# An encoder layer in split fp32 on one core: first loads of the down stages in another order, low parts of the weights on another engine

## The chip, the cores and the metric

The kernel runs on one core of a Trainium2 chip. The metric is the time of one execution on the device in microseconds (us), lower is better. A time of the kernel is the median of three runs. Beside the runs there is one profiled execution, with a trace of every instruction; its times are told from the start of its span.

The engines of the core have these names in the profile: PE is TensorE (PEld its loading of the stationary operand), DVE is VectorE, ACT is ScalarE, POOL is GpSimd, SP is SyncE, which here only issues DMAs. A name with a q behind it (SPq, ACTq) is the DMA queue of that engine.

## The reference

One layer of an encoder is applied to two groups of rows, 256 and 512 tokens (768 rows together), with the same weights. D is 1024, D_FF 2816.

```python
def swiglu(x, w_gu, w_down):
    gate, up = jnp.split(x @ w_gu, 2, axis=-1)
    return (jax.nn.silu(gate) * up) @ w_down
...
x = layer_norm(DN_ALPHA * x + 0.5 * swiglu(x, ffn1_w_gu[l], ffn1_w_down[l]), ln_g[l, 0], ln_b[l, 0])
x = layer_norm(DN_ALPHA * x + parallel_mixer(x, w_mix_in[l], ...), ln_g[l, 1], ln_b[l, 1])
x = layer_norm(DN_ALPHA * x + memory_cross_attention(x, mem, xa_w_q[l], xa_w_kv[l], xa_w_o[l]), ln_g[l, 2], ln_b[l, 2])
x = layer_norm(DN_ALPHA * x + 0.5 * swiglu(x, ffn2_w_gu[l], ffn2_w_down[l]), ln_g[l, 3], ln_b[l, 3])
```

The mixer joins a short convolution and a chunked gated linear attention in two directions; the cross attention reads 256 rows of memory for each group. All values are fp32.

## The kernel before, in words

**Split operands.** Each fp32 operand is split into a high part (a copy in a shorter format, made by ScalarE, L87) and a low part (the operand less its high part, a subtraction, L88). A product is then three matmuls: high by high, high by low, low by high. `split` (L86) does this; its last argument names the engine of the subtraction, VectorE if none is given. In the trace wh and wl are the two parts of a weight, whatever the weight, and raw is the tile that it was loaded to.

**Plain weights.** `load_w` (L90) loads a weight of 128x1024 through SP into one of three shared buffers "raw", and splits it into one of five wh and one of five wl. Without an argument its low part is made by GpSimd. The mixer, the cross attention and `down_last` take their weights from it; some of their calls name VectorE (LO_K, LO_V, every second one in `down_last`). Gate and up weights don't go through it.

**The FFN.** The gate and up projections of the 22 blocks of 128 hidden columns are computed by a scheme of seven products for a two by two block product (`seven`, matmuls at L472, sums of weights and of x as operands). The result of a block, h, is split into hq (kept in SBUF for the last blocks, and spilled to DRAM as hspill, L570). For every pair of blocks that the down stage treats in the same way, `gated` (L559) forms four sums of quarters of h, hs (L575 to L578), and spills them as sspill (L582).

**The down stage.** `down_seven` (L221) does four pairs of blocks with seven products each, over quadrants B11, B21, B12, B22 of the down weight. The pair (9,10) comes first, since its h is still in SBUF (`keep`). For each pair d, P1(d) multiplies B11 by a quarter of h into the banks x, and P2(d) B21 by another into the banks z; the order is P1(0), P2(0), P1(1), P2(1), P1(2), P2(2), P2(3), P1(3). Then the results are added to the accumulators acc by VectorE (L294, L296), and the sum products follow: for each pair the quadrant B12 is added to a copy T of B11 (L331) and the result multiplied by a spilled sum, `summed` (sr, split into ao). Two more rounds of sum products end the function. The spilled quarters of h come through `direct` into a ring of four buffers ao. One product is 18 matmuls of 512 columns, named dn at L284. Afterwards `down_last` (L355) does the remaining pairs and the layer norm.

**Where quadrants are loaded to.** `loaded` (L241) takes turns: of five loads two go to raw7 tiles of the stage's own pool and three to the shared raw. The stage's pool lies in memory that the gate and up stage uses until its end. B11 of the pairs d = 0 and 1 is loaded twice: once as a weight, and later again into T for the sums.

**What sets the order.** The program is written stage by stage, and a scheduler of the framework places the instructions on each engine's queue by their estimated times; each queue then runs in that order. `tc.issue_after(ins)` keeps what is issued within it behind the instruction ins on that instruction's queue; it adds no wait for other engines. SP's queue holds nearly all loads and spills; an instruction on it that waits holds back all loads behind it. `late` collects the spill of the last pair's four sums, which `down_seven` then issues after its products (L323). `load_acc` loads the input rows of the accumulators through ScalarE's queue (L1215). `ahead` (L349) loads h for `down_last` (hr, L653).

Of the kernel before, what the change touches and what calls it, by code (L numbers as in the profile page):

```python
# [7 lines left out]
F32 = mybir.dt.float32  # L8
# [3 lines left out]
ALU = mybir.AluOpType  # L12
# [7 lines left out]
NFB = D_FF // 128  # L20
# [38 lines left out]
def _encoder(ctx, tc, nc, io, out, dbg):  # L59
# [30 lines left out]
    def load_w(src, lo_eng=None, pool=None, in_parts=False):  # L90

        raw = wp.tile([128, 1024], F32, tag="raw", bufs=3, name=nid("raw"))
        h = (pool or wp).tile([128, 1024], F32R, tag="wh", bufs=1 if pool else 5, name=nid("wh"))
        l = (pool or wp).tile([128, 1024], F32R, tag="wl", bufs=1 if pool else 5, name=nid("wl"))
        def part(a, b):
            nc.sync.dma_start(raw[:, a:b], src[:, a:b])
            split(h[:, a:b], l[:, a:b], raw[:, a:b], lo_eng or nc.gpsimd)

        halves = [(h[:, c:c + 512], l[:, c:c + 512]) for c in (0, 512)]
        if in_parts:  # L100
            return halves, part
        part(0, 1024)
        return halves
# [116 lines left out]

    def down_seven(n, wdn, pairs, keep, dr, sd, order6, load_acc, late, ahead):  # L221

        with tc.tile_pool(name=f"seven{n}", bufs=1, reuse_waits="tile") as pool:
            V = nc.vector
            nd = len(pairs)
            raw = [pool.tile([128, 1024], F32, name=nid("raw7")) for _ in range(2)]
            turn = [0]  # L230
            T = {d: pool.tile([128, 1024], F32, name=nid("T")) for d in range(nd)}
# [9 lines left out]
            def loaded(q, d):  # L241
                turn[0] += 1
                if turn[0] % 5 < 2:
                    r = raw[turn[0] % 5]
                else:
                    r = wp.tile([128, 1024], F32, tag="raw", bufs=3, name=nid("raw"))
                quadrant(r[:], q, d)
                return r[:]
# [10 lines left out]
            def direct(t, par, d):  # L259
# [3 lines left out]
                a = ring()  # L263
                kp = pairs[d][0]
                nc.sync.dma_start(a[:].bitcast(F32), dr[:, t, par, kp:kp + 2])
                return [a[:, k] for k in range(2)]

            def summed(s, d):
                r = pool.tile([128, 2, HT], F32, tag="sr", bufs=3, name=nid("sr"))
                kp = pairs[d][0]  # L270
                nc.sync.dma_start(r[:], sd[:, s, kp:kp + 2])
                a = ring()
# [49 lines left out]
            P1(own[-1])  # L322
            for spill in late:  # L323
                spill()
            for d in early:
                quadrant(T[d][:], B11, d)
            load_acc(1, 1)
            add(0, 0, z)
            add(0, 0, x)
            for d in sums_:  # L330
                V.tensor_tensor(T[d][:], T[d][:], loaded(B12, d), op=ALU.add)  # L331
                product(y, summed(0, d), weight(T[d][:]), d == sums_[0], d == sums_[-1])
            load_acc(0, 1)
# [8 lines left out]
            load_acc(1, 0)  # L342
            add(0, 1, y)
            for d in sums_:
                b12, b22 = loaded(B12, d), loaded(B22, d)
                V.tensor_tensor(b12, b12, b22, op=ALU.add)
                product(x, summed(3, d), weight(b12), False, d == sums_[-1])
            add(1, 1, x)
            ahead()  # L349
            for d in own:  # L350
# [160 lines left out]
    def ffn_fast(n, i, front, order6, src, groups, last):  # L511
# [37 lines left out]

        h_of, late = {}, []  # L550

# [7 lines left out]
        def gated(j, h32):  # L559
# [11 lines left out]
            if par and kp not in last:  # L571
# [6 lines left out]
                V.scalar_tensor_tensor(s_[2][:], s_[1][:], -1.0, a12, ALU.mult, ALU.subtract)  # L578

                def spill():  # L580
                    for x in (3, 0, 1, 2):
                        nc.sync.dma_start(sd[:, x, kp, :], s_[x][:])  # L582

                if j == NFB - 1:
                    late.append(spill)
                else:
                    spill()

# [69 lines left out]
        else:  # L658
            lp = hlp.enter_context(tc.tile_pool(name="hlast", bufs=1, reuse_waits="tile"))
            ahead = lambda: load_h(js, lp, "hr", 6)  # L660
        down_seven(n, wdn, groups, keep, dr, sd, order6, load_acc, late, ahead)

# [785 lines left out]
```

## Time and profile before

| | |
|---|---|
| runs | 1814.77, 1810.16, 1815.77 us |
| median | 1814.77 us |
| profiled execution, its own time | 1809.75 us |
| its span | 1808.0 us |
| mean granted clock of TensorE | 0.991 |
| end of the gate and up stage, FFN1 and FFN2 | 336.24 us, 1621.39 us |
| GpSimd's pieces of wl | 94, 231.6 us |

The profile's page gives the busy time of every engine, then the span in 40 slices, the DMA queues, the chain that ended last, the costliest groups of instructions and the DMA issues. A row of the timeline reads: start, duration, engine, line, operation, out<-in, shapes, count; the bracket gives the idle time of the engine before it and what ended it. A row of waits reads: engine and what it was about to do, what released it and from where, then us in total, how often, and the longest. A row of the windows gives, after the stretch, its length, busy time and instructions of PE, PEld, DVE, ACT and POOL, the granted clock (1.00 is full speed), the busy share of the DMA engines and what they moved in GB/s.

### The profile page before, as it was taken

What the parts mean: (1) busy time and instruction counts of PE and PEld (TensorE: products, weight loads), DVE (VectorE), ACT (ScalarE), POOL (GpSimd) and SP (SyncE); (2) the same over time, 40 slices, a digit from 0 to 9 for tenths busy, and PEclk for the clock granted to TensorE, in tenths of its full rate; (3) what the DMA queues carried; (4) which work ended last, traced back from release to release, by engine and by line L of the source; (5) the groups of instructions that cost most, each with busy time, mean ns of one, the idle gap of its engine ahead of it and who ended that gap; (6) DMA issues with size and microseconds to landing.
All of it is one profiled execution on the core that took longest, in us unless ns stands there. A gap on an engine that the chain in (4) does not pass through costs nothing. (4 is left out here: it accounts for less than half of the span.)

```text
span 1808.0 us, 25217 instructions
## 1 busy us (share of the span) xinstructions
PE 1762.3 (97%) x9758; PEld 1618.6 (90%) x9758; DVE 1216.4 (67%) x2035; ACT 763.8 (42%) x1297; POOL 321.7 (18%) x186
## 2 busy tenths in 40 slices
PE   9999999899999999999999999999999999988998
PEld 9999999788889999888888888889899999986886
DVE  8777777377579553577664934585697777754856
ACT  6444454243135544645322244235344444432421
POOL 2000000000224002422244253244430000000012
PEclk9999999899999999999999999999999999998999
DMA  5434333597432333311463252255424343329951
GB/s 193 143 128 157 135 134 104 186 344 253 185 105 94 123 132 125 104 47 41 132 213 117 83 192 66 80 186 176 140 96 154 128 144 131 127 85 346 334 179 70
DMA packets 100535, 267.26 MB, mean 148 GB/s; under 512 B 10016, under 2 KB 23584, under 8 KB 100416
## 3 DMA queue, kind: packets, MB, share of 16 engines
q1 hardware_dynamic: 93504, 250.46, 39.9%
q10 hardware_dynamic: 6912, 15.21, 2.3%
q8 instruction: 76, 1.25, 0.3%
q14 instruction: 43, 0.35, 0.1%
HBM read 212.15 MB, written 53.48 MB: 147 GB/s over the span
## 5 line engine op out<-in xcount | busy, mean ns | idle before, releaser
L88 POOL TENSOR_TENSOR wl<-raw,wh 128x1024 fp32r<-128x1024 f32 (+1 forms) x94 | 231.6, 2468 | 1319.7 <-ACT wh L87 1271.4
L87 ACT ACTIVATE wh<-raw 128x512 fp32r<-128x512 f32 (+2 forms) x309 | 255.5, 830 | 330.0 <-PE to L108 81.6
L88 DVE TENSOR_TENSOR wl<-raw,wh 128x512 fp32r<-128x512 f32 (+2 forms) x215 | 182.8, 853 | 99.6 <-ACT wh L87 99.3
L284 PE MATMUL dn<-wh,ao 128*128 128x512 f32 x600 | 185.4, 389 | 0.0
L106 PE MATMUL pt<-xh,wh 128*128 128x512 f32 (+2 forms) x512 | 173.1, 338 | 0.0
L107 PE MATMUL pt<-xl,wh 128*128 128x512 f32 (+2 forms) x512 | 172.3, 337 | 0.0
L108 PE MATMUL pt<-xh,wl 128*128 128x512 f32 (+2 forms) x512 | 172.0, 336 | 0.0
L284 PEld LDWEIGHTS dn<-wh,ao 128*128 128x128 f32 x600 | 112.6, 188 | 23.5
L87 ACT ACTIVATE wh<-tt 128x512 fp32r<-128x512 f32 x156 | 95.3, 625 | 78.8 <-PE px L472 36.7
L284 PE MATMUL dn<-wl,ao 128*128 128x512 f32 x300 | 116.7, 389 | 0.0
L88 DVE TENSOR_TENSOR wl<-tt,wh 128x512 fp32r<-128x512 f32 x156 | 105.5, 689 | 2.2 <-ACT wh L87 0.5
L106 PEld LDWEIGHTS pt<-xh,wh 128*128 128x128 f32 x512 | 97.0, 189 | 9.7 <-issue 0.5
L108 PEld LDWEIGHTS pt<-xh,wl 128*128 128x128 f32 x512 | 97.0, 189 | 9.0
L107 PEld LDWEIGHTS pt<-xl,wh 128*128 128x128 f32 x512 | 97.1, 190 | 8.8 <-issue 0.2
L472 PE MATMUL px<-xh,wl 128*128 128x384 f32 x232 | 77.5, 334 | 0.0
L472 PE MATMUL px<-xh,wh 128*128 128x384 f32 x232 | 77.5, 334 | 0.0
L472 PE MATMUL px<-xl,wh 128*128 128x384 f32 x232 | 77.5, 334 | 0.0
L545 DVE SCALAR_TENSOR_TENSOR h<-sil,sum 128x384 f32<-128x384 f32 x78 | 43.5, 557 | 47.1 <-ACT sil L544 47.1
L544 ACT ACTIVATE sil<-sum 128x384 f32<-128x384 f32 x39 | 20.5, 526 | 125.9 <-DVE sum L484 125.9
L284 PEld LDWEIGHTS dn<-wl,ao 128*128 128x128 f32 x300 | 56.3, 188 | 11.8
L106 PE MATMUL dn<-wh,hr 128*128 128x512 f32 (+1 forms) x150 | 57.7, 385 | 0.0
L107 PE MATMUL dn<-wl,hr 128*128 128x512 f32 (+1 forms) x150 | 57.5, 383 | 0.0
(374 smaller groups left out, 4866.4 us busy)
## 6 DMA issues: line engine op xcount, KB each, us to landing
raw<-in_ffn_gu_dram SPq DMA_DIRECT2D x84, 512.0 KB, 3.5
raw<-in_ffn_dn_dram SPq DMA_DIRECT2D x64, 512.0 KB, 5.2
hspill<-hq SPq DMA_DIRECT2D x24, 768.0 KB, 3.7
raw<-in_w_mix_dram SPq DMA_DIRECT2D x32, 512.0 KB, 3.5
ao<-hspill SPq DMA_DIRECT2D x18, 768.0 KB, 5.7
sspill<-hs SPq DMA_DIRECT2D x64, 192.0 KB, 2.1
sr<-sspill SPq DMA_DIRECT2D x32, 384.0 KB, 5.7
hr<-hspill SPq DMA_DIRECT2D x24, 384.0 KB, 5.6
```

The source lines that it names most:

```text
L87: nc.scalar.activation(hi, src, AF.Copy)
L88: (lo_eng or nc.vector).tensor_tensor(lo, src, hi.bitcast(F32), op=ALU.subtract)
L106: nc.tensor.matmul(o, lh, rh, start=start, stop=False)
L107: nc.tensor.matmul(o, lh, rl, start=False, stop=False)
L108: nc.tensor.matmul(o, ll, rh, start=False, stop=stop)
L284: nc.tensor.matmul(ps[t][:], l, r[:, o], start=start and k == 0 and m == 0, stop=stop and k == 1 and m == 2, skip_group_check=True)
L472: nc.tensor.matmul(ps, l[:, c], r[:, k, :], start=st and n == 0, stop=sp_ and n == 2, skip_group_check=True)
L544: nc.scalar.activation(sil[:], g, AF.Silu)
L545: ins = nc.vector.scalar_tensor_tensor(h32[:, half * HT:(half + 1) * HT], sil[:], -0.5, u, ALU.mult, ALU.mult)
```

## The change

It has four parts. In `load_w` the low part of a plain weight is made by VectorE wherever GpSimd made it. In `loaded` the turns of raw7 and the shared raw are shifted, so that the first three loads of a down stage go to the shared buffers and the fourth and fifth to raw7. The four spills of the last pair's sums are issued in `gated` on ScalarE's queue; the list `late` is gone. The reloads of B11 into T and the first round of sum loads are kept behind the last load of a spilled quarter on SP's queue, and stand in the program after the additions to acc; the loads of h for `down_last` are kept behind the last load of the second round of sums.

```diff
-            split(h[:, a:b], l[:, a:b], raw[:, a:b], lo_eng or nc.gpsimd)
+            split(h[:, a:b], l[:, a:b], raw[:, a:b], lo_eng)
...
             def loaded(q, d):
                 turn[0] += 1
-                if turn[0] % 5 < 2:
-                    r = raw[turn[0] % 5]
+                if turn[0] % 5 in (4, 0):
+                    r = raw[turn[0] % 5 // 4]
                 else:
                     r = wp.tile([128, 1024], F32, tag="raw", bufs=3, name=nid("raw"))
...
-                nc.sync.dma_start(a[:].bitcast(F32), dr[:, t, par, kp:kp + 2])
+                last_load[0] = nc.sync.dma_start(a[:].bitcast(F32), dr[:, t, par, kp:kp + 2])
...
-                nc.sync.dma_start(r[:], sd[:, s, kp:kp + 2])
+                last_load[0] = nc.sync.dma_start(r[:], sd[:, s, kp:kp + 2])
...
             P1(own[-1])
-            for spill in late:
-                spill()
-            for d in early:
-                quadrant(T[d][:], B11, d)
             load_acc(1, 1)
             add(0, 0, z)
             add(0, 0, x)
-            for d in sums_:
-                V.tensor_tensor(T[d][:], T[d][:], loaded(B12, d), op=ALU.add)
-                product(y, summed(0, d), weight(T[d][:]), d == sums_[0], d == sums_[-1])
+
+            with tc.issue_after(last_load[0].ins):
+                for d in early:
+                    quadrant(T[d][:], B11, d)
+                for d in sums_:
+                    V.tensor_tensor(T[d][:], T[d][:], loaded(B12, d), op=ALU.add)
+                    product(y, summed(0, d), weight(T[d][:]), d == sums_[0], d == sums_[-1])
...
+            hold = last_load[0].ins
             for d in sums_:
...
-            ahead()
+            with tc.issue_after(hold):
+                ahead()
...
-                def spill():
-                    for x in (3, 0, 1, 2):
-                        nc.sync.dma_start(sd[:, x, kp, :], s_[x][:])
-
-                if j == NFB - 1:
-                    late.append(spill)
-                else:
-                    spill()
+                queue = nc.scalar if j == NFB - 1 else nc.sync
+                for x in (3, 0, 1, 2):
+                    queue.dma_start(sd[:, x, kp, :], s_[x][:])
```

Three places show how the queues change. The first is SP's queue at the start of the down stage of FFN1. The first rows here are the last spills of an earlier pair; raw and raw7 are tiles for quadrants, ao a spilled quarter of h, hs597 to hs600 the sums of the last pair. Before:

```order
L582 DMA sspill1_84<-hs543_3141 128x384
L238 DMA raw625_3550<-in_ffn1_dn_dram 128x2x512
L582 DMA sspill1_84<-hs600_3438 128x384
L582 DMA sspill1_84<-hs597_3435 128x384
L582 DMA sspill1_84<-hs598_3436 128x384
L582 DMA sspill1_84<-hs599_3437 128x384
L238 DMA raw7602_3459<-in_ffn1_dn_dram 128x2x512
L265 DMA ao621_3524<-hspill1_83 128x1536
L265 DMA ao624_3548<-hspill1_83 128x1536
L238 DMA T605_3462<-in_ffn1_dn_dram 128x2x512
```

And after the change, from the same spill on:

```order
L582 DMA sspill1_84<-hs543_3141 128x384
L237 DMA raw621_3527<-in_ffn1_dn_dram 128x2x512
L237 DMA raw635_3630<-in_ffn1_dn_dram 128x2x512
L264 DMA ao622_3529<-hspill1_83 128x1536
L264 DMA ao625_3553<-hspill1_83 128x1536
L237 DMA raw7602_3463<-in_ffn1_dn_dram 128x2x512
L237 DMA T605_3466<-in_ffn1_dn_dram 128x2x512
L264 DMA ao628_3579<-hspill1_83 128x1536
```

The raw7 load that is the first product's weight before is the fourth product's after; the weights of the first three stand ahead of it (two of them ahead of these rows), and no spill of the last pair is left on SP.

The second place is VectorE's queue at the beginning of the sum products of FFN1. T is a quadrant that is being summed, dn607 to dn609 are the banks x, dn610 to dn612 the banks z, and ao and wl here are low parts. Before:

```order
L331 TENSOR_TENSOR T604_3461<-T604_3461,raw640_3689 128x1024
L88 TENSOR_TENSOR ao642_3694<-sr641_3692,ao642_3694 128x2x384
L331 TENSOR_TENSOR T605_3462<-T605_3462,raw645_3719 128x1024
L296 SCALAR_TENSOR_TENSOR acc_3454<-acc_3454,dn610_3467 128x512
L88 TENSOR_TENSOR wl644_3698<-T604_3461,wh643_3697 128x1024
L296 SCALAR_TENSOR_TENSOR acc_3454<-acc_3454,dn611_3468 128x512
L296 SCALAR_TENSOR_TENSOR acc_3454<-acc_3454,dn612_3469 128x512
L88 TENSOR_TENSOR ao647_3724<-sr646_3722,ao647_3724 128x2x384
L294 TENSOR_TENSOR acc_3454<-acc_3454,dn607_3464 128x512
```

And after the change:

```order
L295 SCALAR_TENSOR_TENSOR acc_3458<-acc_3458,dn610_3471 128x512
L295 SCALAR_TENSOR_TENSOR acc_3458<-acc_3458,dn611_3472 128x512
L295 SCALAR_TENSOR_TENSOR acc_3458<-acc_3458,dn612_3473 128x512
L330 TENSOR_TENSOR T604_3465<-T604_3465,raw641_3690 128x1024
L293 TENSOR_TENSOR acc_3458<-acc_3458,dn607_3468 128x512
L293 TENSOR_TENSOR acc_3458<-acc_3458,dn608_3469 128x512
L88 TENSOR_TENSOR ao643_3695<-sr642_3693,ao643_3695 128x2x384
L293 TENSOR_TENSOR acc_3458<-acc_3458,dn609_3470 128x512
L88 TENSOR_TENSOR wl645_3699<-T604_3465,wh644_3698 128x1024
```

The low part of the first sum's weight (wl644 before, wl645 after) stands ahead of the adds of the banks x before, and behind the last of them after.

The third place is VectorE's queue in the norm of a tile of rows that ends the mixer; wl are low parts of weights of the cross attention, rqt and rqy steps of the norm's inverse square root. Before:

```order
L140 TENSOR_SCALAR rqy1399_9169<-rqi1398_9168 128x1
L142 TENSOR_TENSOR rqt1394_9145<-rqy1393_9144 128x1
L142 TENSOR_TENSOR rqt1400_9170<-rqy1399_9169 128x1
L143 SCALAR_TENSOR_TENSOR rqt1394_9145<-rqt1394_9145,rqa1391_9142 128x1
L143 SCALAR_TENSOR_TENSOR rqt1400_9170<-rqt1400_9170,rqa1397_9167 128x1
L144 SCALAR_TENSOR_TENSOR rqy1393_9144<-rqt1394_9145,rqy1393_9144 128x1
```

And after the change:

```order
L140 TENSOR_SCALAR rqy1400_9170<-rqi1399_9169 128x1
L88 TENSOR_TENSOR wl1426_9351<-raw1424_9349,wh1425_9350 128x1024
L142 TENSOR_TENSOR rqt1395_9146<-rqy1394_9145 128x1
L142 TENSOR_TENSOR rqt1401_9171<-rqy1400_9170 128x1
L143 SCALAR_TENSOR_TENSOR rqt1395_9146<-rqt1395_9146,rqa1392_9143 128x1
L143 SCALAR_TENSOR_TENSOR rqt1401_9171<-rqt1401_9171,rqa1398_9168 128x1
L88 TENSOR_TENSOR wl1432_9386<-raw1430_9384,wh1431_9385 128x1024
L144 SCALAR_TENSOR_TENSOR rqy1394_9145<-rqt1395_9146,rqy1394_9145 128x1
```

Two low parts of weights, on GpSimd before, now stand between the small steps.

More of the change, by code (lines that the diff above doesn't have):

```diff
@@ L219, in down, with down_seven @@
             tok_mm(ps, w, kk, hh[s.name, t, j], hl[s.name, t, j], first and kk == 0, stop and kk == 1, cols)
-    def down_seven(n, wdn, pairs, keep, dr, sd, order6, load_acc, late, ahead):
+    def down_seven(n, wdn, pairs, keep, dr, sd, order6, load_acc, ahead):
         with tc.tile_pool(name=f"seven{n}", bufs=1, reuse_waits="tile") as pool:
@@ L229, in down_seven @@
             raw = [pool.tile([128, 1024], F32, name=nid("raw7")) for _ in range(2)]
-            turn = [0]
+            turn, last_load = [0], [None]
             T = {d: pool.tile([128, 1024], F32, name=nid("T")) for d in range(nd)}
@@ L548, in block @@
             gated(j, h32)
-        h_of, late = {}, []
+        h_of = {}
         def hq_tile(hs):
@@ L660, in ffn_fast @@
             ahead = lambda: load_h(js, lp, "hr", 6)
-        down_seven(n, wdn, groups, keep, dr, sd, order6, load_acc, late, ahead)
+        down_seven(n, wdn, groups, keep, dr, sd, order6, load_acc, ahead)
         with tc.tile_pool(name=f"down{n}", bufs=1, reuse_waits="tile") as f2:
```

## The prediction

> **What bounds the kernel now.** I read the page's head first, then the waits of TensorE, then the timelines of the places that these name.
>
> ```profile
> span 1808.0 us, 25217 instructions
> PE 1762.3 (97%) x9758; PEld 1618.6 (90%) x9758; DVE 1216.4 (67%) x2035; ACT 763.8 (42%) x1297; POOL 321.7 (18%) x186
> ```
>
> TensorE is busy for 1762.3 of 1808.0 us. The change takes no matmul away, so it can only work on the other 45.7 us and on the clock that a pause costs. The waits of TensorE (us in total, times, longest) say where these are:
>
> ```profile
> PE dn L284 <- ACT wh L87: 20.8, 2, 11.9
> PE px L472 <- ACT snap L477: 4.3, 2, 3.5
> PE K L108 <- DVE wl L88: 4.0, 2, 2.3
> PE kv L904 <- DVE uc L973: 1.5, 1, 1.5
> PE pt L107 <- DVE oT L88: 1.4, 1, 1.4
> ```
>
> Almost half of it, 20.8 us, is two waits: one at the start of each down stage. On TensorE's timeline (start, duration, idle before in brackets) they stand so, the first in FFN1, the second in FFN2:
>
> ```profile
> 345.11 1.22 PE L284 MATMUL dn<-wh,hq 128*128 128x512 f32 x2 [8.87 <-ACT wh L87]
> ...
> 348.24 0.63 PE L284 MATMUL dn<-wh,hq 128*128 128x512 f32 x1
> 348.66 0.63 PE L284 MATMUL dn<-wl,hq 128*128 128x512 f32 x1
> ...
> 350.37 0.98 PE L284 MATMUL dn<-wh,hq 128*128 128x512 f32 x2
> ...
> 351.42 0.63 PE L284 MATMUL dn<-wh,hq 128*128 128x512 f32 x2
> 351.89 0.39 PE L284 MATMUL dn<-wl,hq 128*128 128x512 f32 x1
> ...
> 1633.31 1.22 PE L284 MATMUL dn<-wh,hq 128*128 128x512 f32 x2 [11.92 <-ACT wh L87]
> ...
> 1637.30 0.93 PE L284 MATMUL dn<-wh,hq 128*128 128x512 f32 x2
> ```
>
> The pause costs more than itself. Up to 350.37 matmuls begin 0.42 us apart (348.24 to 348.66), afterwards 0.235 apart (two in the 0.47 from 351.42 to 351.89). The windows show why: the granted clock (third figure from the end) is 0.50 after the pause and 1.00 later.
>
> ```profile
> 344.00:348.00 4.00, 2.85 (x6) 1.84 (x7) 2.67 (x3) 3.59 (x4) 0.00 (x0) 0.50 1.00 402
> 356.00:360.00 4.00, 4.00 (x20) 3.27 (x19) 1.81 (x2) 2.12 (x2) 0.00 (x0) 1.00 1.01 377
> 360.00:405.00 45.00, 45.00 (x200) 37.28 (x199) 33.56 (x37) 18.52 (x20) 0.00 (x0) 1.00 0.94 341
> ```
>
> From 345.11 to 350.37 are 5.26 us, in which 12.5 matmuls begin at 0.42; at 0.235 they take 2.9, so the slow clock costs 2.35 us. From 1633.31 to 1637.30 are 3.99 us, 9.5 matmuls, 2.2 at full clock: 1.8 us. Both starts together cost 8.87 + 2.35 + 11.92 + 1.8 = 24.9 us.
>
> What TensorE waits for there is a chain that begins on SP's queue:
>
> ```profile
> 298.60 2.71 SPq L238 DMA_DIRECT2D raw<-in_ffn_dn_dram  x2
> ...
> 323.63 16.65 SPq L582 DMA_DIRECT2D sspill<-hs  x4
> 340.39 0.38 SPq L238 DMA_DIRECT2D raw<-in_ffn_dn_dram  x1
> 340.89 0.89 SPq L265 DMA_DIRECT2D ao<-hspill  x2
> ...
> 339.39 0.55 DVE L578 SCALAR_TENSOR_TENSOR hs<-hs,h 128x384 f32<-128x384 f32 x1
> ...
> 344.00 1.06 ACT L87 ACTIVATE wh<-raw 128x1024 fp32r<-128x1024 f32 x1 [5.70 <-DMA raw<-in_ffn_dn_dram]
> ...
> 1626.76 0.38 SPq L238 DMA_DIRECT2D raw<-in_ffn_dn_dram  x1
> ...
> 1632.20 1.06 ACT L87 ACTIVATE wh<-raw 128x1024 fp32r<-128x1024 f32 x1 [8.76 <-DMA raw<-in_ffn_dn_dram]
> ```
>
> Two weights of the stage are loaded at 298.60, long before, but they belong to its second and later products. The weight of the first product goes into a tile of the down stage's own pool. It is issued at 340.39, behind four spills that hold SP until the last hs is made (339.94), then takes 3.6 us to land and 1.1 to split.
>
> **The change part by part.**
>
> *Tiles of the first loads, and their place on SP.* In the new order the first three weights go to the shared raw buffers and stand on SP where the two of 298.60 stand now. Their splits come before the SiLU of the last two blocks on ScalarE. So the first product starts when the last gate/up matmul ends: 345.11 − 8.87 = 336.24, and 1633.31 − 11.92 = 1621.39. That removes the 24.9 us, clock loss included, if no new pause takes their place. On ScalarE three splits of 1.06 us come before the end of the gate/up stage; nothing on TensorE waits for ScalarE there now, so they cost 0, or at most 3.2 us per stage if each stood on the path.
>
> *What comes late next: the spilled operands.* The next product that needs new data from the queue is the third, by its ao. Its memory is that of hs, so it cannot be issued before 339.94; today it is issued at 340.89. The first two products have their operands (h in SBUF). Eight products run from 345.11 to the first add of their last bank:
>
> ```profile
> 377.13 1.22 DVE L88 TENSOR_TENSOR wl<-T,wh 128x1024 fp32r<-128x1024 f32 x1
> ...
> 380.33 0.68 DVE L294 TENSOR_TENSOR acc<-acc,dn 128x512 f32<-128x512 f32 x1
> ```
>
> That is 35.2 us, less 2.35 for the clock, or 4.1 each. The third then wants its ao at 336.24 + 8.2 = 344.4 and the fourth its weight and ao at 348.5. The load that was issued at 340.39 landed 3.6 us later, and the page's median for ao is 5.7 (below); that gives 343.6 to 345.7 for the third. So the wait is 0 to 1.3 us there, perhaps 0.7 more at the fourth, whose weight still has to be split: 0 to 2, and I take 1 in FFN1. In FFN2 the first ao does not depend on hs; I take 0.
>
> *The clock in so short a wait.* The two waits of K in the list above, 2.3 us at most, are in a window whose clock is 1.00 (1170 to 1215, below), so I charge a wait of 2 us itself and nothing more. "TensorE: Matmul & The Clock Gate" of the Trainium skill, Part 1, says that the array goes to half clock after an idle window of about 3.4 us; this agrees with the trace at 8.87 and at 2.3. It adds that the window runs freely, so a pause is not judged from its own start; by that rule a 2 us wait beside another short gap could still cost the 1.8 to 2.35 us again, and the sum would be that much worse once per stage.
>
> *The spills of the last pair, now on ScalarE's queue.* They free SP from the 16.65 us hold; the instructions behind them there are acc loads and the split of the fourth product's weight. That weight lands after 343 and hs is done at 339.94, so nothing waits: 0.
>
> *The start of the sum products.* Here the new order loses something. On VectorE the low part of the first sum's weight (wl, 1.22 us, at 377.13 today) now stands behind all adds of the accumulators, the last of which needs the end of the eighth product. So TensorE will wait for one add and one wl, 0.68 + 1.22, and their semaphores: 2 to 2.5 us in each stage; I take 2.5. The floor is 0, if the scheduler's queue leaves the first matmuls on wh something to do meanwhile. The reloads of T now come behind the last ao. By bytes:
>
> ```profile
> raw<-in_ffn_dn_dram SPq DMA_DIRECT2D x64, 512.0 KB, 5.2
> ...
> ao<-hspill SPq DMA_DIRECT2D x18, 768.0 KB, 5.7
> sspill<-hs SPq DMA_DIRECT2D x64, 192.0 KB, 2.1
> sr<-sspill SPq DMA_DIRECT2D x32, 384.0 KB, 5.7
> ```
>
> From 340 on come six ao, four weights, four spills and six acc pieces (256 KB each) before the reloads: 9.2 MB. Then come two T, one raw and one sr, 2.0 MB. At 390 GB/s, between the 377 and 402 of the windows, 11.2 MB take 28.7 us and are there at 368.7. The eighth product ends at 336.24 + 32.8 + 1 = 370. So the data are there, with 1 us to spare.
>
> *Low parts on VectorE.* It gets the 94 pieces that GpSimd has now:
>
> ```profile
> L88 POOL TENSOR_TENSOR wl<-raw,wh 128x1024 fp32r<-128x1024 f32 (+1 forms) x94 | 231.6, 2468 | 1319.7 <-ACT wh L87 1271.4
> ...
> 1009.25 5.21 POOL L88 TENSOR_TENSOR wl<-raw,wh 128x1024 fp32r<-128x1024 f32 x2 [22.09 <-ACT wh L87]
> ...
> 1009.77 2.36 DVE L143 SCALAR_TENSOR_TENSOR rqt<-rqt,rqa 128x1 f32<-128x1 f32 x1
> ...
> 1020.25 0.23 DVE L143 SCALAR_TENSOR_TENSOR rqt<-rqt,rqa 128x1 f32<-128x1 f32 x2
> ...
> 990.00:1035.00 45.00, 43.25 (x259) 38.51 (x258) 41.58 (x113) 9.86 (x12) 12.57 (x5) 1.00 0.19 60
> 1170.00:1215.00 45.00, 42.72 (x292) 39.56 (x292) 42.17 (x86) 16.27 (x20) 17.46 (x8) 1.00 0.44 152
> ```
>
> On VectorE a piece takes 1.22 us, so 94 are at most 115 us on an engine that is busy for 1216.4. But GpSimd's pieces hold VectorE up today: a step of one element per partition, 0.12 us each at 1020.25, lasts 2.36 us when it starts beside a GpSimd piece, to the end of that piece. The two fullest windows of VectorE (its figure stands behind those of PE and PEld) take on 5 and 8 pieces, 6.1 and 9.8 us, and lose about 2.2 for each piece that met such a step. If each did, they come out lower by 4.9 and 7.8; if none did, they need 47.7 and 52.0 of 45 us, 9.7 too many. So the waits of K, kv and oT (6.9 us in the list) may all go, or 9.7 come. K's waits are nearest to the held steps; I take a gain of 2.5, most of their 4.0. The other stages have VectorE under 42 of 45 and TensorE full: 0.
>
> **The rivals.**
>
> *The feed decides.* TensorE begins 8.9 us earlier while the large loads begin at 340 as before. For it speaks the DMA share of 1.00 in the windows, and the mean of 341 GB/s in 360 to 405. "DMA: Bandwidth & Descriptors" of the Trainium skill, "Issuing engines are not separate DMA queues", is on its side: what ScalarE issues runs on the same engines, and only issue time is saved. At 341 GB/s the 11.2 MB take 32.9 us; the first sum comes 4.2 us later in each stage and some 0.8 more is lost on the way: 10 us less gain, 1802. Against it: that mean holds stretches in which SP waited for buffers.
>
> *VectorE's queue becomes the bound, slower.* The place is the mixer and the attention, where the low parts now stand between the steps of the norms: VectorE's instructions run in order, so a moved piece whose wh isn't made yet holds back all behind it. GpSimd waited 1271 us for ScalarE without harm; VectorE can't. A late weight costs TensorE 2.0 us (K: 4.0 in 2). Ten such among the 94 eat the gain of 19 us at the starts, thirteen make the kernel measurably slower, eighteen give 1814 − 19 + 36 = 1831. Against it: VectorE is at 67%, and where K's own pieces are made there today it waits twice only.
>
> *More comes back in the middle.* All 6.9 us of short waits go, and the sums start without the 2.5 each: 1792 − 4.4 − 5 = 1783.
>
> *The first loads don't get ahead*, for instance because the shared buffers come free too late. The same buffers take two loads at 298.60 today, so I hardly believe it. The starts would cost what they cost now, and only the middle remains: 1811.
>
> **How the numbers follow.** Starts 24.9, less 1 for the feed and 2 × 2.5 at the sums, is 18.9; with 2.5 in the middle, 21.4. The profiled execution took 1809.75 (span 1808.0), so its like would take 1788.4. The three runs of before (1814.77, 1810.16, 1815.77) have a mean of 1813.6, 3.8 above it; with this I predict 1792. Chances: forecast 0.70, feed 0.11, more in the middle 0.11, no gain at the starts 0.04, slower 0.04. The range reaches from the third to the first rival, 1782 to 1803. A measurement of this kernel tells 0.3% (5.4 us) from no change. Faster 0.92, same 0.04, slower 0.04.
>
> **What would show it.** Right: no wait above 2.5 us at the starts of the down stages and a clock of 1.00 through them; waits of dn for VectorE's wl of about 2.5 us at the sums; 2.36 us steps of L143 gone; VectorE near 1216 + 115 − 60. Wrong: an 8 us wait that remains or moves to an ao, a clock of 0.5 after it, or a list of new waits for wl in the mixer and the attention that adds up to more than 10 us.

## The result and the profile after

The changed kernel takes 1780.62 us (median of four runs, 1780.23 to 1781.46), the kernel before 1813.39 in the same series (1810.16 to 1815.77). The ratio is 0.9821, 95% interval 0.9804 to 0.9838. That is 1.4 us below the range of the prediction (1782 to 1803) and 11.4 below its value: the sign was right, the gain was half as large again as forecast.

The head of the profile of the changed kernel:

```profile
span 1778.4 us, 25213 instructions
PE 1757.9 (99%) x9758; PEld 1615.4 (91%) x9758; DVE 1257.3 (71%) x2127; ACT 766.4 (43%) x1297; POOL 96.0 (5%) x94
```

TensorE is without work for 20.5 us instead of 45.7. GpSimd falls from 321.7 to 96.0. VectorE took on 92 pieces but rose by 41 us only; the other two of GpSimd's 94 pieces are of gate and up weights and stay there. TensorE's waits after the change (us in total, times, longest):

```profile
PE dn L283 <- DVE wl L88: 3.3, 4, 1.3
PE px L473 <- ACT snap L478: 2.5, 1, 2.5
PE warm L75 <- POOL ident masks.py:199: 2.3, 1, 2.3
PE o L922 <- DVE st L907: 1.1, 1, 1.1
PE dn L283 <- ACT wh L87: 1.1, 2, 0.6
PE dn L283 <- DMA ao<-hspill: 0.9, 1, 0.9
PE py L473 <- ACT snap L478: 0.6, 1, 0.6
```

The 20.8 us in front of the down products are gone. The waits of K, kv and oT, 6.9 us before, are all missing, and so is one of 0.8 us of the mixer's last products. Most of the new waits lie where the prediction put them. On TensorE's timeline they are at the third (in FFN1 alone), the fourth and the ninth product of a down stage:

```profile
345.65 0.50 PE L283 MATMUL dn<-wh,ao 128*128 128x512 f32 x1 [0.91 <-DMA ao<-hspill]
350.54 0.97 PE L283 MATMUL dn<-wh,ao 128*128 128x512 f32 x3 [0.52 <-ACT wh L87]
351.80 0.50 PE L283 MATMUL dn<-wl,ao 128*128 128x512 f32 x1 [0.29 <-DVE wl L88]
373.84 0.50 PE L283 MATMUL dn<-wl,ao 128*128 128x512 f32 x1 [1.34 <-DVE wl L88]
1616.58 0.96 PE L283 MATMUL dn<-wh,ao 128*128 128x512 f32 x3 [0.58 <-ACT wh L87]
1639.89 0.50 PE L283 MATMUL dn<-wl,ao 128*128 128x512 f32 x1 [1.35 <-DVE wl L88]
```

SP issues the first spilled quarter when the sums are done (340.0 us), and the granted clock (third figure from the end) stays full through the start:

```profile
340.08 0.81 SPq L264 DMA_DIRECT2D ao<-hspill  x2
340.99 0.46 SPq L237 DMA_DIRECT2D raw<-in_ffn_dn_dram  x1
```

```profile
344.00:348.00 4.00, 3.09 (x14) 2.25 (x13) 0.00 (x0) 0.00 (x0) 0.00 (x0) 1.00 1.02 406
348.00:352.00 4.00, 3.18 (x13) 2.01 (x13) 1.40 (x2) 2.12 (x2) 0.00 (x0) 1.00 1.04 420
```

For the comparison I cut each trace in three, at the end of the last gate and up matmul and at the last matmul of `down_seven`, in FFN1 and FFN2. "Middle" is all between the first down stage and the second: `down_last` of FFN1, mixer, cross attention, gate and up of FFN2. The table holds all traces of this study (us). The runs come from five series, in which the kernel before has medians of 1811.3 to 1813.6; so a difference of 2 us between medians of different series says little.

| kernel | low parts by | down, FFN1 | middle | down, FFN2 | median of runs |
|---|---|---|---|---|---|
| before | GpSimd | 126.7 | 1158.4 | 129.2 | 1813.39 |
| before, second trace | GpSimd | 125.8 | 1159.8 | 130.7 | 1811.49 |
| after | VectorE | 119.1 | 1148.1 | 118.0 | 1780.62 |
| after, second trace | VectorE | 119.3 | 1148.1 | 116.5 | 1780.08 |
| low parts alone | VectorE | 125.7 | 1147.3 | 129.2 | 1798.11 |
| down stages alone | GpSimd | 119.0 | 1162.6 | 116.8 | 1794.12 |
| turns alone | GpSimd | 120.7 | 1160.6 | 122.4 | 1799.89 |
| old turns | VectorE | 126.0 | 1148.2 | 123.5 | 1791.84 |
| spills on SP | VectorE | 120.3 | 1148.1 | 119.6 | 1783.45 |
| GpSimd reads besides | VectorE | 119.1 | 1196.5 | 117.6 | 1831.03 |
| GpSimd sets besides | VectorE | 119.8 | 1151.2 | 118.2 | 1783.94 |
| additions behind, acc later | VectorE | 121.4 | 1151.1 | 119.7 | 1786.13 |
| additions behind | VectorE | 119.2 | 1148.1 | 117.7 | 1783.58 |
| additions of x late | VectorE | 119.1 | 1147.3 | 116.8 | 1780.30 |

From the first trace of before to that of after, the down stages gained 7.6 and 11.2 us, 18.8 together, where the prediction had 18.9. The middle gained 10.3, where it had 2.5.

### The profile page after: what moved, and what is told of

The parts are those of the page before. It is cut to its first block, busy times and chain, and to the rows that moved or that the text cites. A ratio compares the mean times of both kernels' runs of the same rounds, so it can differ in the third digit from the quotient of the medians.

```text
span 1778.4 us, 25213 instructions
## 1 busy us (share of the span) xinstructions
PE 1757.9 (99%) x9758; PEld 1615.4 (91%) x9758; DVE 1257.3 (71%) x2127; ACT 766.4 (43%) x1297; POOL 96.0 (5%) x94
## 4 chain that ended last, share of the span: by engine, by line
PE 89%; DVE 5%; DMA 2%; POOL 1%; ACT 1%; issue 1%; SPq 0%; DVEq 0%; ACTq 0%; POOLq 0%
PE px L473 22%; PE py L473 11%; PE dn L283 11%; PE pz L473 6%; PE pt L106 5%; PE pt L107 5%; PE pt L108 5%; PE to L106 2%; PE to L108 2%; PE to L107 2%; PE dn L106 2%; PE dn L108 2%; PE dn L107 2%; POOL mS4l L88 1%; DVE wl L88 1%; PE K L108 1%
## 5 line engine op out<-in xcount | busy, mean ns | idle before, releaser
L88 DVE TENSOR_TENSOR wl<-raw,wh 128x512 fp32r<-128x512 f32 (+2 forms) x307 | 290.1, 947 | 167.7 <-ACT wh L87 167.0
L545 ACT ACTIVATE sil<-sum 128x384 f32<-128x384 f32 x39 | 20.5, 525 | 118.8 <-DVE sum L485 118.8
L175 POOL TENSOR_TENSOR acc<-acc,ln_b 128x512 f32<-128x512 f32 x14 | 18.6, 1354 | 875.9 <-ACT acc L174 875.9
```

What stands on the lines that cost most here:

```text
L88: (lo_eng or nc.vector).tensor_tensor(lo, src, hi.bitcast(F32), op=ALU.subtract)
L175: nc.gpsimd.tensor_tensor(Ah, Ah, b[h][:], op=ALU.add)
L545: nc.scalar.activation(sil[:], g, AF.Silu)
```

## The experiments

My theory after the result: the parts are independent; the down stages gain by the tile of the first loads; the middle gains because GpSimd no longer holds up VectorE. Rivals for the middle: a low part is simply ready sooner; the raw buffers come free sooner; or the order moved with the down stages.

**Low parts alone.**

```diff
--- before
-            split(h[:, a:b], l[:, a:b], raw[:, a:b], lo_eng or nc.gpsimd)
+            split(h[:, a:b], l[:, a:b], raw[:, a:b], lo_eng)
```

> The kernel before with one part of the change: low parts of plain weights by the vector engine; the down stages as before. From the two traces: the stretch from the end of the first down stage to the end of the second gate and up stage takes 1158.4 us before and 1148.1 after, the two down stages 126.7 and 129.2 before, 119.1 and 118.0 after. Theory: the parts are independent and the 10.3 us of the middle come from this one alone. Then the middle is 1148 here, the down stages stay at 126.7 and 129.2, and the whole is about 10 us under the kernel before (ratio 0.994). Rival: the middle got shorter because the stages before it ended earlier or because the order moved with the down stages; then the middle stays near 1158 and the whole near the kernel before.

1798.11 us, ratio 0.9925 (0.991 to 0.994). The middle takes 1147.3, the down stages still begin with their pauses. In the waits of TensorE those of K, kv and oT are gone, those of the down products are not:

```profile
PE dn L284 <- ACT wh L87: 21.4, 2, 12.4
```

So the whole gain of the middle comes from this part, and it doesn't need the other.

**Down stages alone.** The same line, the other way round, in the changed kernel.

> The changed kernel with GpSimd making the low parts of plain weights again; the down stages as changed. Theory: down stages 119.1 and 118.0 us, middle 1158, the whole 19 us under the kernel before (ratio 0.9896). Rival (the parts depend on each other): the down stages lose part of the gain without the faster low parts, or the middle gets shorter here too.

1794.12 us, ratio 0.9904 (0.9889 to 0.9919). The down stages are as short as with the whole change. The middle, 1162.6, is longer than before, by 4 us. Its waits are those of before within 0.3, but for the one of the mixer's last products, which is 1.74 instead of 0.77. What came on top is the clock: 0.82 and 0.75 behind the wait of kv, and behind this one 0.57, where the trace of before shows 1.00.

```profile
954.82 0.50 PE L106 MATMUL to<-wh,xh 128*128 128x512 f32 x1 [1.74 <-ACT xh L87]
```

```profile
956.00:960.00 4.00, 4.00 (x13) 3.13 (x12) 3.95 (x4) 2.18 (x5) 2.25 (x1) 0.57 0.17 64
824.00:828.00 4.00, 2.46 (x25) 2.27 (x25) 3.78 (x7) 2.59 (x4) 0.18 (x3) 0.82 0.00 0
828.00:832.00 4.00, 4.00 (x31) 3.68 (x29) 2.96 (x9) 3.14 (x8) 0.00 (x0) 0.75 0.00 0
```

**GpSimd reads besides.** VectorE still makes every low part. GpSimd subtracts once more into the raw tile, when nobody needs that any more.

```diff
--- after
             split(h[:, a:b], l[:, a:b], raw[:, a:b], lo_eng)
+            if lo_eng is None:
+                nc.gpsimd.tensor_tensor(raw[:, a:b], raw[:, a:b], h[:, a:b].bitcast(F32), op=ALU.subtract)
```

> The changed kernel, and beside each plain weight whose low part the vector engine makes, GpSimd subtracts once more in place, after the vector engine has read the tile: 92 subtractions of about 2.4 us that nobody needs, except that the raw buffer is freed after them. Theory (hold): steps of the vector engine with two inputs in SBUF last until GpSimd's subtraction ends, and this is what the middle lost before. Then steps of 0.12 us last about 2.4 us again, the short waits of TensorE come back, and the middle takes 1158 us or more: with the low parts themselves now on the vector engine too, 5 to 20 us over the changed kernel. Rival (length of the piece): the middle got shorter because a low part is ready 1.2 us sooner; then it stays at 1148 here. Second rival (buffers): it got shorter because the raw buffer is freed sooner; then this run and the one with memsets lose alike.

1831.03 us, ratio 1.0113 (1.0092 to 1.0134): slower than the kernel before, and 50 us over the changed one. The middle takes 1196.5. Rows of VectorE and then of GpSimd in the norm behind the mixer show the hold: a step of one element per partition lasts until GpSimd's subtraction beside it ends (1016.58 + 2.40 = 1018.98, 1020.54 + 2.37 = 1022.91).

```profile
1016.55 2.44 DVE L145 SCALAR_TENSOR_TENSOR rqt<-rqt,rqa 128x1 f32<-128x1 f32 x2
1020.62 2.31 DVE L146 SCALAR_TENSOR_TENSOR rqy<-rqt,rqy 128x1 f32<-128x1 f32 x1
```

```profile
1016.58 2.40 POOL L99 TENSOR_TENSOR raw<-raw,wh 128x1024 f32<-128x1024 f32 x1 [20.93 <-DVE rqt L144]
1020.54 2.37 POOL L99 TENSOR_TENSOR raw<-raw,wh 128x1024 f32<-128x1024 f32 x1 [1.57 <-DVE rqt L144]
```

The short waits are back and longer:

```profile
PE K L110 <- DVE wl L88: 7.2, 2, 4.9
PE sc L110 <- DVE ql L88: 5.4, 4, 2.8
PE kv L901 <- DVE uc L970: 5.2, 3, 3.9
```

The 48 us are more than twice what I had allowed. Part of them is the clock: the mean granted clock of the profiled execution is 0.989, against 0.998 in the changed kernel. The first rival can't explain this run, in which no low part is made by GpSimd. Nor does it fit the trace of before: after the start of the program TensorE waits there for GpSimd only 0.2 us in all, for a part of another product (mS4l), and never for a wl.

**GpSimd sets besides.** The same place with three memsets instead.

```diff
+                for _ in range(3):
+                    nc.gpsimd.memset(raw[:, a:b], 0.0)
```

> As the run with GpSimd's extra subtractions, but with three memsets of the raw tile in place of the subtraction: GpSimd is busy for about 2.9 us per weight (a memset of 128x768 takes 0.73 us in the trace), the raw buffer is freed at least as late, and GpSimd reads nothing. Hold theory: no step of the vector engine is held, the middle stays at 1148 to 1150. Second rival (buffers): the middle loses as much as with the subtractions. The Trainium skill, SBUF: State Buffer, section SBUF: two separate sides, says that an operation of the vector engine with two SBUF inputs is shut out only by a GpSimd operation that reads SBUF; by that rule the memsets cost nothing.

1783.94 us, ratio 0.9845 (0.983 to 0.986). The middle takes 1151.2: 3.1 over the changed kernel, 1.2 more than I had allowed, and 45 less than with the subtractions. GpSimd was as busy (276 memsets), and the step that shows the hold is at its short time. The groups of GpSimd's memsets and of that step, here, then with the subtractions, then in the kernel before (instructions, busy time, mean in ns):

```profile
L100 POOL MEMSET raw<- 128x1024 f32 x276 | 261.8, 956 | 1276.9 <-DVE wl L88 836.4 <-DMA raw<-in_ffn_dn_dram 382.4 <-issue 22.4
```

```profile
L146 DVE SCALAR_TENSOR_TENSOR rqt<-rqt,rqa 128x1 f32<-128x1 f32 x48 | 6.5, 156 | 0.3
```

```profile
L145 DVE SCALAR_TENSOR_TENSOR rqt<-rqt,rqa 128x1 f32<-128x1 f32 x48 | 19.2, 421 | 0.3
```

```profile
L143 DVE SCALAR_TENSOR_TENSOR rqt<-rqt,rqa 128x1 f32<-128x1 f32 x48 | 16.8, 374 | 0.4
```

So neither a busy GpSimd nor late raw buffers explain the middle; the buffers may explain the 3 us. What holds VectorE here is GpSimd's subtraction, which reads SBUF, and not its memset, which only writes. The Trainium skill, "SBUF — State Buffer", "SBUF: two separate sides", says that an operation of VectorE with two SBUF inputs is shut out only by a GpSimd operation that reads SBUF, and these two runs agree with it.

**Old turns.**

```diff
--- after
-                if turn[0] % 5 in (4, 0):
-                    r = raw[turn[0] % 5 // 4]
+                if turn[0] % 5 < 2:
+                    r = raw[turn[0] % 5]
```

> The changed kernel with the old turns of loaded: the first weight of a down stage goes to a raw7 tile of the stage's own pool again; spills and holds stay as changed, and no spill stands ahead of that load on SP's queue. Theory (tile): the tile is the cause, since its memory comes free only when the gate and up stage ends. Then each down stage begins with a pause of at least the 3.6 us of the load and the 1.1 of its split, 5 to 9 us, followed by a granted clock of 0.5, and the whole is 10 to 20 us over the changed kernel. Rival (queue): the spills on SP were the cause; then with the spills on the scalar engine's queue there is no pause beyond 2 us.

1791.84 us, ratio 0.9889 (0.9872 to 0.9905), 11.2 over the changed kernel. Both stages begin with a pause again, the first here and the second equally long:

```profile
341.50 1.22 PE L283 MATMUL dn<-wh,hq 128*128 128x512 f32 x2 [5.22 <-ACT wh L87]
```

The pause is 5.22 and not 8.87 or 11.9, but the reason that the theory gave is not what the trace shows. SP issues the load to the raw7 tile at 330.10, and it lands 3.7 us later, before the last gate and up matmul ends (336.27). So the memory of this tile is not held until the end of that stage. What is late is the split: on ScalarE's queue it stands behind the last pair's spills, which the change put there and which wait for their sums. In FFN2 the split stands behind them in the same way, at 1614.58, the product at 1615.69.

```profile
330.10 0.38 SPq L237 DMA_DIRECT2D raw<-in_ffn_dn_dram  x1
```

```profile
338.08 2.27 ACTq L582 DMA_DIRECT2D sspill<-hs  x3
340.39 1.06 ACT L87 ACTIVATE wh<-raw 128x1024 fp32r<-128x1024 f32 x1 [2.06 <-DMA sspill<-hs]
```

In the kernel before it is the load that stands behind these spills, on SP; here it is the split, on ScalarE. Either way the first product waits for the last sums. The new turns help because the load and the split of the first weight then stand ahead of the spills. The raw7 tile with no spill ahead of its load or its split was not run; by these times (330.10 + 3.7 + 1.1 = 334.9) its weight would be ready in time.

**Turns alone.** The opposite edit to the kernel before.

> The kernel before with the new turns of loaded alone; spills of the last pair late on SP, reloads and loads of h not held back, low parts on GpSimd. Theory: the pause of 8.9 and 11.9 us at the starts goes as with the whole change. But in the order of SP two sum weights and two to three loads of h (0.4 MB each) now stand ahead of the first spilled quarter, some 2 MB, 5 us at 390 GB/s; so the third product waits about 5 us in each down stage where the changed kernel waits 0.9, and the gain at the starts is 18.9 less 8 to 10. Rival: these loads are issued while the queue waits for the sums anyway and cost nothing; then the down stages are as short as in the run of the down stages alone (119.0 and 116.8 us).

1799.89 us, ratio 0.9932 (0.9916 to 0.9948). The pause at the first product is gone, but the third waits:

```profile
349.64 0.80 PE L284 MATMUL dn<-wh,ao 128*128 128x512 f32 x1 [4.26 <-DMA ao<-hspill]
```

The same wait of FFN2 is 4.40. I had expected about 5. The holds on SP's queue and the moved spills bring it to 0.9 and less; against the run of the down stages alone they are worth 1.7 us in FFN1 and 5.6 in FFN2.

**Spills on SP.**

```diff
--- after
-                queue = nc.scalar if j == NFB - 1 else nc.sync
+                queue = nc.sync
```

> The changed kernel with the four spills of the last pair on SP's queue again, in the order of the others; nothing else differs on any queue. Theory: no load that is needed early stands behind them, since the first spilled quarter has to wait for the same sums; 0 to 1 us per stage. Rival: SP held by the spills delays the quarters and the fourth weight; then the third product waits 2 us or more longer, 4 us or more in all. The Trainium skill, DMA: Bandwidth & Descriptors, section Issuing engines are not separate DMA queues, says that only the issue time is saved by another queue; four issues of 0.4 to 0.6 us would by that be about 2 us per stage at most.

1783.45 us, ratio 0.9849 (0.9827 to 0.9872). The third product waits 1.92 and 1.97, where the changed kernel has 0.91 and none: 3 us in all, between theory and rival.

```profile
346.75 0.50 PE L283 MATMUL dn<-wh,ao 128*128 128x512 f32 x1 [1.92 <-DMA ao<-hspill]
```

In FFN1 the first quarter is issued at 340.57 instead of 340.08, one issue later. In FFN2 it needs none of the last sums, and the changed kernel issues it at 1597.30, before the end of the gate and up stage (1603.47). Here SP's queue holds it behind spills that wait for their sums, until 1609.26, after that end (1604.81). The changed kernel's row, then those of this run:

```profile
1597.30 0.34 SPq L264 DMA_DIRECT2D ao<-hspill  x1
```

```profile
1606.60 2.25 SPq L582 DMA_DIRECT2D sspill<-hs  x3
1609.26 0.82 SPq L264 DMA_DIRECT2D ao<-hspill  x2
```

The Trainium skill ("DMA: Bandwidth & Descriptors", "Issuing engines are not separate DMA queues") says that another issuing engine saves just the time of issue. The half microsecond of FFN1 is of that size. FFN2 goes beyond it: the other queue spares SP the wait for the sums, more than 10 us, of which 1.97 reach TensorE.

**Additions behind, acc later.** Can the remaining waits go? In the changed kernel the additions of both sets of banks were kept behind the low parts of the first sum, and the first acc pieces loaded two pairs later.

```diff
-                if d == 0:
+                if d == 2:
                     load_acc(0, 0)
...
+                    if d == sums_[0]:
+                        with tc.issue_after(low[0].ins), tc.issue_after(low[1].ins):
+                            add(0, 0, z)
+                            add(0, 0, x)
```

> The changed kernel with two edits: the additions of the first two sets of banks are kept behind the low parts of the first sum's weight and operand on the vector engine, and the first three pieces of acc are loaded two pairs later. Theory: the waits of the down products for the vector engine's wl, 1.3 us at the start of the sums in each stage, go; the waits for the first spilled quarter and the fourth weight, 0.9 + 0.5 + 0.3 and 0.6 + 0.3, shrink by up to 2 us of transfer (0.8 MB at 390 GB/s). In all 2.5 to 5 us under the changed kernel. Rival: the additions now collide with the second sum's low parts, or the late acc pieces hold the additions; then nothing is gained or up to 3 us lost.

1786.13 us, ratio 0.9857 (0.9841 to 0.9873), 5.5 over the changed kernel: the rival. The waits for the quarter and the fourth weight went, but at the sums VectorE now waits for the load, which shares the DMA engines (share 1.03 to 1.05 from 352 to 372) with the late acc pieces:

```profile
368.17 1.23 DVE L328 TENSOR_TENSOR T<-T,raw 128x1024 f32<-128x1024 f32 x1 [6.77 <-DMA raw<-in_ffn_dn_dram]
```

TensorE waits 1.89 and 1.58 there. The middle is 3 us longer with nothing moved in it that matters, and the clock shows why. The window behind the wait of o (1.12 us) is here at 0.58 and 0.57, and at 1.00 in the changed kernel, where the wait is also 1.12:

```profile
868.00:872.00 4.00, 4.00 (x23) 2.65 (x23) 3.58 (x7) 2.44 (x5) 0.00 (x0) 0.58 0.11 15
872.00:876.00 4.00, 4.00 (x13) 3.15 (x12) 2.98 (x14) 0.64 (x1) 0.00 (x0) 0.57 0.86 254
```

```profile
868.00:872.00 4.00, 4.00 (x24) 3.23 (x23) 3.63 (x6) 2.51 (x4) 0.00 (x0) 1.00 0.37 103
872.00:876.00 4.00, 4.00 (x25) 3.51 (x24) 3.61 (x13) 0.00 (x0) 0.00 (x0) 1.00 0.87 268
```

**Additions behind**, with the acc pieces where the changed kernel has them.

> The changed kernel with one edit, half of the run before: the additions of the first two sets of banks stand behind the low parts of the first sum's weight and operand on the vector engine; acc is loaded where the changed kernel loads it. Theory: the run with both edits lost because the late acc pieces pushed the first sum's weight back in a stretch where the DMA share is 1.0 (its load landed 8.9 us after issue, and the add to T began at 368.2). With acc early again the data are there, the wait of 1.3 us at the start of the sums goes or shrinks in each stage, and the whole is 1 to 3 us under the changed kernel. Rival: the additions, now behind, hold the second sum's low parts; then waits of 1 to 2 us appear at the second sum and nothing is gained.

1783.58 us, ratio 0.985 (0.9833 to 0.9866): nothing gained. The wait of the first sum shrank to 0.58 and 0.26, and one of 0.99 and 0.95 appeared at the second: the rival again.

**Additions of x late.** Only the additions of the banks x go behind, and behind two sums.

```diff
--- after
-            add(0, 0, x)
...
+                    if d == sums_[1]:
+                        with tc.issue_after(low[0].ins), tc.issue_after(low[1].ins):
+                            add(0, 0, x)
```

> The changed kernel with one edit: of the additions at the start of the sums only those of the banks x, the last of which waits for the end of the eighth product, are kept behind the low parts of the first two sums' weights and operands on the vector engine; those of the banks z stay where they are. Theory: the low part of the first sum's weight then waits for nothing of the eighth product, the 1.3 us wait at the start of the sums goes in each stage without coming back at the second sum, and the whole is 2 to 3 us under the changed kernel (1780.6), below both kernels. Rival: the sum's operands come too late from DRAM anyway (in the run with all additions behind, 0.6 and 1.0 us of waits for wl stayed); then at most 1 us is gained.

1780.30 us (1777.87 to 1781.22), ratio 0.9818 (0.9805 to 0.9832). The waits at the sums went as meant, 0.41 and 0.30 for 1.34 and 1.35:

```profile
374.34 0.50 PE L283 MATMUL dn<-wl,ao 128*128 128x512 f32 x1 [0.41 <-DVE wl L88]
```

But the two waits before them in FFN1 were 1.50 and 1.09 in this execution, and the median can't be told from the changed kernel's 1780.08 to 1780.62. No version tried is surely better than the changed kernel.

**Second traces of both kernels.**

> The kernel before, unchanged, for a second trace. Theory (clock by chance): short waits of 1 to 2.3 us sometimes are followed by a stretch at a granted clock of 0.5 to 0.8 and sometimes not, depending on when they fall. Then this trace has the same short waits in the middle as the first (kv 1.5, oT 1.4, K 1.8 and 2.3, within 0.3), but drops of the clock behind some of them, or behind others, and a middle that differs from 1158.4 by 1 to 4 us. Rival: the clock behind a short wait is the same in every execution, and the middle is 1158.4 within 0.5.

> The changed kernel, unchanged, for a second trace. Theory (clock by chance): it has one wait over 0.7 us in the middle (o, 1.1 us) and so little to lose; the middle is 1148.1, or up to 2 us more if the clock drops behind that one. Rival: 1148.1 within 0.5 in any case.

1811.49 and 1780.08 us. The kernel before has the same short waits within 0.2; its middle is 1.4 longer, with a drop of the clock behind the wait of kv that the first trace doesn't have:

```profile
832.00:836.00 4.00, 2.29 (x26) 1.90 (x24) 3.88 (x7) 3.25 (x7) 0.18 (x3) 0.89 0.00 0
836.00:840.00 4.00, 4.00 (x25) 3.90 (x25) 3.65 (x12) 3.90 (x6) 0.00 (x0) 0.68 0.00 0
```

The changed kernel's middle is 1148.1 both times.

## Why the prediction was right and wrong

**The starts of the down stages: right, the total in part by luck.** The pause and its slow clock (24.9) went. The prediction read it as a load held on SP behind the last pair's spills, and the run with the old turns bears that out; that the tile lies in the stage's own pool plays no part, its memory being free at 330.10. For the feed I took 1 us and it cost 0.91 + 0.52 + 0.29 in FFN1 and 0.58 + 0.30 in FFN2, where I took none. For the sums I took 2.5 each and they cost 1.34 and 1.35, for the reason given: first the add on the last bank, then wl. VectorE's rows in the changed kernel show this order, and that the load was in time, the add to T beginning at 368.38 with no wait for a DMA:

```profile
368.38 1.22 DVE L330 TENSOR_TENSOR T<-T,raw 128x1024 f32<-128x1024 f32 x1
...
371.96 0.68 DVE L293 TENSOR_TENSOR acc<-acc,dn 128x512 f32<-128x512 f32 x1
372.56 1.22 DVE L88 TENSOR_TENSOR wl<-T,wh 128x1024 fp32r<-128x1024 f32 x1
```

The two errors work against each other: with these waits the gain would be 24.9 less 5.3, 19.6, where the prediction had 18.9 and the traces show 18.8. The missing 0.8 stays open. The feed rival at 341 GB/s did not come: the windows of the start moved 406 and 420.

**Low parts on VectorE: the step that failed.** "K's waits are nearest to the held steps; I take a gain of 2.5, most of their 4.0." The mechanism was the one named, the size was off by four: 10.3 in the first pair of traces. Nearness in the list was a poor guide. I had looked for holds in the norms alone. But in the trace of before such a step stands right in front of the wait of oT as well: three pieces of 128x512 took 3.07 us beside GpSimd's wl, which ended at 915.42.

```profile
913.85 3.07 DVE L88 TENSOR_TENSOR oT<-sig,oT 128x512 fp32r<-128x512 f32 x3
```

```profile
913.05 2.37 POOL L88 TENSOR_TENSOR wl<-raw,wh 128x1024 fp32r<-128x1024 f32 x1 [6.25 <-ACT wh L87]
```

In the changed kernel one of these pieces takes 0.68. In front of kv it is the 128x1536 product of L1013, 3.84 us at 824.28 in before, 1.76 on average in after. So K, kv and oT (6.9) all went, and with them the wait of 0.8 in the mixer's last products and about 1 of the 1.7 at the start of FFN2's seven products (0.82 and 0.88 before, 0.61 after). These are 8.8 of the 10.3; the rest is not in the list of waits and stays open. My range for this step, 9.7 lost to 6.9 gained, left the last two of these out. VectorE's total confirms the size of the hold: 1216.4 + 92 pieces of 1.235 would be 1330; it is 1257.3, so 73 us of held time went where I had put 60.

**The clock in a short wait: wrong.** "I charge a wait of 2 us itself and nothing more" was read from one execution in which no drop happened to follow. (Of the two waits of K that it names, one is at 1034.32, outside the window that it points to; the clock was 1.00 there too.) Waits of 1.1 to 2.3 us in the middle were followed by clocks of 0.57 to 0.89 in four other traces (before again, down stages alone, turns alone, acc later), and by 1.00 in others with the same wait. Over the four traces with GpSimd's pieces (before twice, down stages alone, turns alone) the middle is 1158.4 to 1162.6, 1160.4 on average; over the seven with VectorE's and no extra work, leaving out the run with that drop behind o, 1147.3 to 1148.2, 1147.9 on average. So the part is worth 12.5, or 12.1 with that run kept in, of which the first pair of traces showed 10.3. The prediction had cited the Trainium skill's free-running window ("TensorE: Matmul & The Clock Gate", Part 1) for a sum that would be worse; it should have taken that as a rival with a price. The page speaks of an idle window of about 3.4 us; here a drop came 2 us after a wait of 1.12 us, the only gap of TensorE's in the 4 us before it, and the measurement decides. When such a wait brings a drop and when not stays open.

**The 3.8 us from the profile to the runs: wrong.** I carried over that the runs of before lay 3.8 above its profiled execution. That distance did not come along: before runs from 1808.6 to 1816.5 in all series, after from 1779.3 to 1781.5, and its profiled execution (1780.23) stands among its runs. The second trace of before is longer than the first by 1.4 us in the middle and by 1.5 at the start of the second down stage, both stretches that the change shortens. But another 1.5 lie in the first gate and up stage, which the change hardly touches (its end is at 337.75 instead of 336.24), and after's second trace has 1.8 more there too (338.13 instead of 336.32). So the two traces explain the 3.8 only in part: 2.0 of it would be the middle, 1160.4 on average where the first trace has 1158.4. The rest stays open. The 7.8 that were missing in the middle and these 3.8 make 11.6, against a miss of 11.4.

**The rivals.** "More comes back in the middle" was the nearest, at 1783 with 0.11; its mechanism is what happened, though the sums kept half of their wait. VectorE's queue did not become the bound: its waits for wh rose from 110.1 to 175.5 us in total, and no new wait of TensorE in the mixer or the attention is longer than 0.3. The stalls of the slower rival do appear when GpSimd reads beside it (1831.03, its 1831 by chance).

## What to carry to other kernels

GpSimd's subtractions held steps of VectorE with two inputs that ran beside them; moving them onto VectorE, busy for 67%, shortened VectorE's critical chains. So add up held steps over the whole trace, in front of every wait, before pricing such a move. A prefetch is only as early as its place on the queues: look at what stands ahead of the first load of a stage on its queue, and then at what stands ahead of its split on the next one. A short wait of TensorE has a price of its own and a chance of a slow clock; one trace shows one draw, and the other executions of the same kernel need not repeat it.

## What was not expected

- Low parts on both engines at once cost more than the sum suggests: the middle rose by 48 us with 92 subtractions whose results nobody needs, where I had bounded it by 20.
- Three memsets of 956 ns each in the same places, more GpSimd time than the subtractions (261.8 against 239.5 us), cost 3 us.
- The clock fell to 0.57 behind a wait of 1.12 us, and stayed at 1.00 behind the same wait in other executions.
- The runs of one series scatter by 1.2 us in after and with the low parts alone, by 5.1 to 7.0 in before and by 7.4 with the extra subtractions. GpSimd's pieces alone don't explain it: with the spills on SP it is 5.1, with the down stages alone, where GpSimd makes the pieces, 2.5.
